# The two halves of a split weight in one buffer, at ten offsets: a TensorE-bound encoder on one core

## The chip, the core and the metric

One core of one Trainium2 chip runs the kernel. The metric is the time of one execution on the device, in microseconds (us). Two runs of the kernel before took 962.38 and 962.40 us, median 962.39. Engines are called as the profile calls them: PE (TensorE, matmuls), PEld (TensorE's weight loads), DVE (VectorE), ACT (ScalarE), POOL (GpSimd) and SP (SyncE, which issues the transfers).

## The reference

A trunk of two encoder layers over 256 tokens of width 1024, float32 throughout. In each layer the normed input is multiplied by one wide matrix, feeds four branches (latent attention, a short gated convolution, a convolution module with 31 taps, chunked spatial gating), and the branches are merged by sigmoid gates:

```
h = rms_norm(x, norm_mix_pre[l])
proj = h @ w_in[l]
...
merged = g[:, :, 0] * y_a + g[:, :, 1] * y_b + g[:, :, 2] * y_c + g[:, :, 3] * y_d
x = x + rms_norm(merged @ w_out[l], norm_mix_post[l])
h2 = rms_norm(x, norm_ffn_pre[l])
gu = h2 @ w_ffn_in[l]
f_g, f_u = jnp.split(gu, 2, axis=-1)
f = (jax.nn.silu(f_g) * f_u) @ w_ffn_out[l]
x = x + rms_norm(f, norm_ffn_post[l])
```

Nearly all of the work is products of the 256 tokens with some 83 MB of weights in each layer, each of which is read once.

## The kernel before, in words

**Weights come in units.** `unit_list` (line 46) cuts each layer's weights into 80 units of up to 128 x 2048 words. A unit is fetched by SP into a buffer `raw` (4 of them), and then split by `Weights.split` (line 345) into two float32r halves: ACT rounds `raw` to `hi` (line 356), DVE takes the rest, `lo = raw - hi` (line 357). There are five buffers for `hi` and five for `lo`, each of 2048 words, and unit number i uses the i-th of them in turn. The activations are split in the same way (`hth`/`htl` for the normed input, `fh`/`fl`, `mh`/`ml` and others for what follows).

**Products come in threes.** `group` (line 390) multiplies high by high, high by low and low by high into one bank of PSUM; each matmul has a weight load of its own (the stationary operand), and streams the other operand past it (the moving one, which is named first in the profile, as `pb<-hi,hth`). Two ways of use matter here:

- In most units the weights are moving: 512 words of `hi` or `lo` are streamed past 128 columns of activations. The first three units of a layer (`compressed`, line 659) stream 272 words at a time, and one unit (`w_uq`) 384.
- In the units of `w_in` with all 1024 rows (`b_unit`, line 534: 256 columns of one of the convolution, gating or short-convolution inputs) the weights are stationary: 128 columns of `hi` or `lo` are loaded, and 256 words of `hth` or `htl` streamed.

**Where the operands lie.** In the program as built, `hth`, `htl`, every `raw`, `hi` and `lo` buffer and every 512-word slot begins 64 bytes behind a multiple of 256 bytes in its partition. So a moving block of 512 or 256 words and the weights that are loaded for it begin at the same place in a line of 256 bytes: their distance, as it is called below, is 0 bytes modulo 256. Only the units of 544 columns depart from it: their blocks of 272 words are 1088 bytes long, and block k, half n begins 2176k + 1088n bytes into the buffer, so with three rows of blocks the distances run 0, 64, 128, 192, 0, 64, and with two (the third such unit) 0, 64, 128, 192.

**The order of the work** is written out by a planner in the kernel itself: it keeps a clock with an estimated cost for each instruction and picks, engine by engine, what is issued next (classes and functions from line 168 on; every ACT, DVE and POOL instruction is recorded at line 176). Side work (transposes, attention, the convolution) is slipped between the big products. Small columns of one to six words (`small`, line 287) go round through rings of eight buffers for each width.

Of the kernel before, what the change touches and what calls it, by code (L numbers as in the profile page):

```python
# [11 lines left out]
F32 = mybir.dt.float32  # L12
F32R = mybir.dt.float32r
# [5 lines left out]
P = 128  # L19
L = 2  # L20
D = 1024
# [10 lines left out]
EPS = 1e-6  # L32
NCOL = 148
UW = 2048
FIRST = 544

O_CQ, O_CKV, O_KR = 0, 256, 512
# [59 lines left out]
def hybrid_encoder(ctx: ExitStack, tc: tile.TileContext, wts, x_in, pos, invf, cols, rows, wst, out):  # L97
# [62 lines left out]
    class Engine:  # L160
        def __init__(self, eng, key, cost):
            self.eng, self.key, self.cost = eng, key, cost
# [102 lines left out]
    wp = ctx.enter_context(tc.tile_pool(name="wp", bufs=1))  # L265
    sb = ctx.enter_context(tc.tile_pool(name="sb", bufs=1))
    ps = ctx.enter_context(tc.tile_pool(name="ps", bufs=1, space=bass.MemoryType.PSUM))

    B_RAW, B_HI, B_SLOT, B_BIG, B_GAIN = 4, 5, 25, 2, 2
# [7 lines left out]
    def nm(s):  # L277
        cnt[0] += 1
        return f"{s}_{cnt[0]}"
# [5 lines left out]
        return sb.tile([P, D], F32, tag="big", name=nm(s), bufs=B_BIG)  # L285

    def small(n, s="c"):
        return sb.tile([P, n], F32, tag=f"c{n}", name=nm(s), bufs=8 if n < 8 else 4)

    rings = {"pb": [], "psd": []}  # L290

# [30 lines left out]
    units = unit_list()  # L322
# [3 lines left out]
        offs.append(offs[-1] + w)  # L326
    NU = len(units)

    class Weights:
        def __init__(self):  # L330
            self.nd = self.ns = self.n = self.nf = 0
# [2 lines left out]
        def load(self, i, t=0.0):  # L334
            l, u = divmod(i, NU)
            w, after = widths[u], t
            t = wp.tile([P, UW], F32, tag="raw", name=nm("raw"), bufs=B_RAW)
            o = (l * offs[-1] + offs[u]) * P
            src = wts[o : o + w * P].rearrange("(p w) -> p w", w=w)
            step = FIRST if i == 0 else w  # L340
            for c in range(0, w, step):
# [2 lines left out]

        def split(self, i):
            w = widths[i % NU]
            h = wp.tile([P, UW], F32R, tag="hi", name=nm("hi"), bufs=B_HI)
            lo = wp.tile([P, UW], F32R, tag="lo", name=nm("lo"), bufs=B_HI)
            raw = self.raw.pop(i)
            step = FIRST if i == 0 else 1024  # L350
            self.parts[i] = (h, lo)
            spans = [(c, min(w, c + step)) for c in range(0, w, step)]

            def rank():
                return 0 if i <= self.n + NEAR else 3

            for c, e in spans:
                act.copy(h[:, c:e], raw[:, c:e], rank=rank)
                dve.tensor_tensor(lo[:, c:e], raw[:, c:e], h[:, c:e], op=ALU.subtract, rank=rank, then=self.more if e == w else None)
# [89 lines left out]

    pii = sb.tile([P, T], I32, tag="pii", name="pii")  # L450
    fr = small(16, "fr")

    def tables():
# [5 lines left out]
    def rope_tables():  # L459
        pi = small(T, "pi")  # L460
        dve.tensor_copy(pi, pii)
        ang = small(T * 16, "ang")
        n = small(T * 16, "n")
        for t in range(T):
            dve.tensor_scalar(ang[:, t * 16 : (t + 1) * 16], fr, pi[:, t : t + 1], None, op0=ALU.mult)
        magic = 12582912.0
        dve.tensor_scalar(n, ang, float(np.float32(1.0 / (2 * math.pi))), None, op0=ALU.mult)
        dve.tensor_scalar(n, n, magic, None, op0=ALU.add)
        dve.tensor_scalar(n, n, magic, None, op0=ALU.subtract)
        c1 = 6.28125  # L470
        c2 = math.floor((2 * math.pi - c1) * 2**20) / 2**20
        c3 = 2 * math.pi - c1 - c2
        for c in (c1, c2, c3):
            dve.scalar_tensor_tensor(ang, n, -c, ang, op0=ALU.mult, op1=ALU.add)
        lim = 3.1415925
        dve.tensor_scalar(ang, ang, lim, -lim, op0=ALU.min, op1=ALU.max)
        act.activation(sin.rearrange("p t f -> p (t f)"), ang, AF.Sin)
        dve.scalar_tensor_tensor(n, ang, -1.0, ang, op0=ALU.mult, op1=ALU.max)
        dve.tensor_scalar(n, n, -1.0, math.pi / 2, op0=ALU.mult, op1=ALU.add)
        act.activation(cos.rearrange("p t f -> p (t f)"), n, AF.Sin)  # L480
# [4 lines left out]
    def pre_norm(t, g):  # L485
        h = big()
        ss = small(2)
        s1 = small(1)
        r = small(1)
        for j in range(2):  # L490
            c = slice(512 * j, 512 * (j + 1))
            act.activation(h[:, c], x[:, t, c], AF.Square, scale=D ** -0.5, accum_out=ss[:, j : j + 1], rank=FAST)
            if j == 0:
                pool.tensor_scalar(s1, ss[:, 0:1], EPS, None, op0=ALU.add, rank=FAST)
        rstd_of(r, ss[:, 1:2], s1, rank=FAST)
        for j in range(2):
            c = slice(512 * j, 512 * (j + 1))
            dve.scalar_tensor_tensor(h[:, c], x[:, t, c], r, g[:, c], op0=ALU.mult, op1=ALU.mult, rank=FAST)

        def turn():  # L500
            for j in range(2):
                yield need(h)
                b = sbank()
                transposes(b, [h[:, 512 * j + P * k : 512 * j + P * (k + 1)] for k in range(4)])
                bv = b.rearrange("p (k n) -> p k n", n=P)
                split(hth[:, t, 4 * j : 4 * j + 4, :], htl[:, t, 4 * j : 4 * j + 4, :], bv, FAST)

        return turn()
# [87 lines left out]
    def layer(l):  # L596
# [26 lines left out]
        def mla_tr(t, cn):  # L623
            yield need(cn)
            b = sbank()
            transposes(b, [cn[:, P * k : P * (k + 1)] for k in range(4)])
            for j in range(2):
                o = slice(t * P, (t + 1) * P)
                split(ft2(qc[j])[:, :, o], ft2(ql[j])[:, :, o], b[:, 256 * j : 256 * (j + 1)].rearrange("p (f n) -> p f n", f=2))
# [85 lines left out]
        def split_op(name, j, src):  # L715
            hi, lo = slot(F32R, name + "h"), slot(F32R, name + "l")
            split(hi, lo, src)
            ops[name][j] = (ft2(hi), ft2(lo))
# [481 lines left out]
```

## Time and profile before

| | before |
|---|---|
| median of two runs | 962.39 us |
| the profiled execution's own time | 962.84 us |
| its span, first to last instruction | 961.0 us |
| PE busy | 949.9 us (99%) |
| DVE busy | 669.8 us (70%) |
| ACT busy | 478.5 us (50%) |
| mean granted clock of TensorE | 0.998 of 2.4 GHz |

The profiled execution took 0.45 us longer than the median; 1.84 us of it lie outside the span. Matmuls are pipelined: a row of the profile gives a matmul's time from its start to the end that is modelled for it (389 ns for 512 columns), which overlaps the next one. What one matmul costs is read from the distance between two starts, so a stretch of equal matmuls is priced by its first and last start and their number.

### The profile page before, as it was taken

The page shows a single profiled execution, that of the slowest core. Times are in us where ns is not written, and L with a number is a line of the kernel's source. Part 1 is how long each engine was busy: PE and PEld are TensorE (multiplying, and loading weights), DVE is VectorE, ACT ScalarE, POOL GpSimd, SP SyncE. Part 2 cuts the span into 40 slices and gives each one's busy share as a digit, 9 for nine tenths or more (in the row PEclk, how much of TensorE's full clock was granted, in tenths as well). Part 3 has the DMA queues.
Part 4 walks back from the last instruction along what each step waited for, and adds up shares of the span by engine and source line. Part 5 has one row for each costly group of instructions (what it writes and reads, how often), then busy time and mean ns, then how long its engine had stood idle before and what let it go on. Part 6 is the DMA issues. An engine that isn't in the chain of part 4 may idle for free.

```text
span 961.0 us, 12988 instructions
## 1 busy us (share of the span) xinstructions
PE 949.9 (99%) x5098; PEld 821.4 (85%) x5098; DVE 669.8 (70%) x1018; ACT 478.5 (50%) x749; POOL 50.9 (5%) x95
## 2 busy tenths in 40 slices
PE   7999999999999999999999999999999999999997
PEld 7999988888888888888899999888888888888885
DVE  5978898898857655563387888798887675555432
ACT  6655654446435644443375655544454554444421
POOL 2200000000002000000041000000000110000000
PEclk9999999999999999999999999999999999999999
DMA  8754353565854555565268154455667366455601
GB/s 342 281 200 137 127 175 139 190 229 186 300 181 176 219 178 190 200 221 173 96 231 296 45 176 164 143 186 187 203 239 258 124 218 249 176 176 182 226 8 44
DMA packets 29869, 179.52 MB, mean 187 GB/s; under 512 B 3696, under 2 KB 3824, under 8 KB 10352
## 3 DMA queue, kind: packets, MB, share of 16 engines
q1 hardware_dynamic: 29808, 178.69, 52.3%
q8 instruction: 40, 0.66, 0.3%
q14 instruction: 21, 0.17, 0.0%
HBM read 177.63 MB, written 1.05 MB: 186 GB/s over the span
## 4 chain that ended last, share of the span: by engine, by line
PE 97%; DMA 1%; issue 1%; DVE 0%; SPq 0%; ACT 0%; POOL 0%; DVEq 0%; POOLq 0%
PE pb L256 77%; PE acc L256 12%; PE psd L260 4%; PE psd L256 2%; PE av L256 1%; DMA raw<-in_wts_dram 1%; SPq L317 0%; DVE lo L176 0%; POOL c L176 0%; ACT hi L176 0%; DVE x L176 0%; DVEq L1196 0%; ACT h L176 0%; POOLq L1196 0%; DVE htl L176 0%
## 5 line engine op out<-in xcount | busy, mean ns | idle before, releaser
L176 DVE TENSOR_TENSOR lo<-raw,hi 128x1024 fp32r<-128x1024 f32 (+4 forms) x321 | 374.5, 1202 | 137.6 <-ACT hi L176 137.5
L176 ACT CAST hi<-raw 128x1024 fp32r<-128x1024 f32 (+4 forms) x321 | 319.3, 1036 | 282.8 <-PE pb L256 132.6
L256 PE MATMUL pb<-hi,hth 128*128 128x512 f32 (+1 forms) x704 | 264.3, 387 | 0.7 <-ACT hth L176 0.5
L256 PE MATMUL pb<-lo,hth 128*128 128x512 f32 (+1 forms) x704 | 259.6, 381 | 0.5 <-DVE lo L176 0.5
L256 PE MATMUL pb<-hi,htl 128*128 128x512 f32 (+1 forms) x704 | 259.4, 381 | 0.4 <-DVE htl L176 0.4
L256 PEld LDWEIGHTS pb<-hi,htl 128*128 128x128 f32 x704 | 128.9, 188 | 26.0 <-DVE htl L176 0.6
L256 PEld LDWEIGHTS pb<-hi,hth 128*128 128x128 f32 x704 | 129.2, 188 | 25.4 <-ACT hi L176 0.7
L256 PEld LDWEIGHTS pb<-lo,hth 128*128 128x128 f32 x704 | 129.1, 188 | 24.5 <-DVE lo L176 0.7
L256 PE MATMUL pb<-hth,hi 128*128 128x256 f32 x384 | 109.9, 286 | 0.0
L256 PE MATMUL pb<-htl,hi 128*128 128x256 f32 x384 | 108.6, 283 | 0.0
L256 PE MATMUL pb<-hth,lo 128*128 128x256 f32 x384 | 108.6, 283 | 0.0
L176 DVE SCALAR_TENSOR_TENSOR yc<-zc,hcol,yc 128x241 f32<-128x241 f32 (+14 forms) x240 | 97.9, 472 | 0.0
L256 PEld LDWEIGHTS pb<-htl,hi 128*128 128x128 f32 x384 | 73.7, 192 | 0.3
L256 PEld LDWEIGHTS pb<-hth,hi 128*128 128x128 f32 x384 | 73.6, 192 | 0.3
L256 PEld LDWEIGHTS pb<-hth,lo 128*128 128x128 f32 x384 | 73.7, 192 | 0.0
L256 PE MATMUL acc<-hi,fh 128*128 128x512 f32 x176 | 68.8, 391 | 0.0
L256 PE MATMUL acc<-hi,fl 128*128 128x512 f32 x176 | 68.5, 389 | 0.0
L256 PE MATMUL acc<-lo,fh 128*128 128x512 f32 x176 | 68.5, 389 | 0.0
L256 PEld LDWEIGHTS acc<-hi,fl 128*128 128x128 f32 x176 | 33.0, 188 | 6.9
L256 PEld LDWEIGHTS acc<-lo,fh 128*128 128x128 f32 x176 | 33.0, 188 | 6.8
L256 PEld LDWEIGHTS acc<-hi,fh 128*128 128x128 f32 x176 | 33.0, 188 | 6.8
L176 POOL TENSOR_SCALAR c<-c 128x1 f32<-128x1 f32 (+1 forms) x20 | 10.7, 534 | 510.2 <-ACT sq L176 474.3
(161 smaller groups left out, 1018.1 us busy)
## 6 DMA issues: line engine op xcount, KB each, us to landing
raw<-in_wts_dram SPq DMA_DIRECT2D x152, 1024.0 KB, 4.8
brow<-in_rows_dram SPq DMA_DIRECT2D x24, 256.0 KB, 5.7
gain<-in_rows_dram SPq DMA_DIRECT2D x8, 512.0 KB, 6.5
raw<-in_wts_dram SPq DMA_DIRECT2D x3, 816.0 KB, 4.6
raw<-in_wts_dram SPq DMA_DIRECT2D x2, 768.0 KB, 6.0
raw<-in_wts_dram SPq DMA_DIRECT2D x2, 544.0 KB, 6.2
out_dram<-x SPq DMA_DIRECT2D x4, 256.0 KB, 2.1
raw<-in_wts_dram SPq DMA_DIRECT2D x3, 272.0 KB, 7.1
```

The source lines that it names most:

```text
L176: o.emit = lambda: f(*a, **k)
L256: nc.tensor.matmul(out, lhsT, rhs, **k)
L260: nc.tensor.transpose(out=out, in_=in_, identity=identity)
```

## The change

A unit's `hi` and `lo` now lie in one buffer `hl` of 2 x 2048 + 64 words, of which there are five. `hi` begins at an offset `at0`, and `lo` 2048 words behind it. The offset comes from a table by the number of the unit modulo five: 8, 12, 20, 24 or 28 words (32, 48, 80, 96 or 112 bytes) for the units that `b_unit` uses as stationary operand, and 2, 4, 12, 56 or 60 words (8, 16, 48, 224 or 240 bytes) for all others. The buffers themselves begin at the same place in a line of 256 bytes as before. The 1280 bytes more in each partition are made room for by rings of six buffers in place of eight for the small columns.

In the program as built, each engine has the same instructions in the same order as before, apart from waits. Since a buffer is now released as a whole, some of ACT's roundings wait for one to six matmuls more than before (those that read the `lo` of the same buffer last), and some of DVE's subtractions for 21 to 48 fewer. PE has eight waits more on matmuls of its own, of which each was issued at least 18 matmuls earlier. Some of the small columns on POOL, ACT and DVE now wait also for the reader of the column six places back in the ring.

```diff
@@ -32,6 +32,7 @@
 UW = 2048
+ROOM = 64
 FIRST = 544
@@ -285,7 +286,7 @@
     def small(n, s="c"):
-        return sb.tile([P, n], F32, tag=f"c{n}", name=nm(s), bufs=8 if n < 8 else 4)
+        return sb.tile([P, n], F32, tag=f"c{n}", name=nm(s), bufs=6 if n < 8 else 4)
@@ -326,6 +327,10 @@
     NU = len(units)
 
+    def phase(i):
+        src, r0, r1, _ = units[i % NU]
+        return ((8, 12, 20, 24, 28) if src == "w_in" and r1 - r0 == D else (2, 4, 12, 56, 60))[i % 5]
+
     class Weights:
@@ -344,8 +349,9 @@
         def split(self, i):
             w = widths[i % NU]
-            h = wp.tile([P, UW], F32R, tag="hi", name=nm("hi"), bufs=B_HI)
-            lo = wp.tile([P, UW], F32R, tag="lo", name=nm("lo"), bufs=B_HI)
+            both = wp.tile([P, 2 * UW + ROOM], F32R, tag="hl", name=nm("hl"), bufs=B_HI)
+            at0 = phase(i)
+            h, lo = both[:, at0 : at0 + UW], both[:, UW + at0 : 2 * UW + at0]
             raw = self.raw.pop(i)
```

## Rows read from the trace of the kernel before

**Rows 1.** The page: span, engines' busy time, clock by slices, chain that ended last.

```profile
span 961.0 us, 12988 instructions
...
PE 949.9 (99%) x5098; PEld 821.4 (85%) x5098; DVE 669.8 (70%) x1018; ACT 478.5 (50%) x749; POOL 50.9 (5%) x95
...
DVE  5978898898857655563387888798887675555432
...
PEclk9999999999999999999999999999999999999999
...
PE 97%; DMA 1%; issue 1%; DVE 0%; SPq 0%; ACT 0%; POOL 0%; DVEq 0%; POOLq 0%
```

**Rows 2.** PE's waits, whole run: us in total, times, longest.

```profile
PE psd L260 <- DVE h L176: 2.0, 1, 2.0
PE warm L260 <- POOL mhalf L176: 1.3, 1, 1.3
PE pb L256 <- DVE lo L176: 0.5, 1, 0.5
PE pb L256 <- ACT hth L176: 0.5, 1, 0.5
PE pb L256 <- DVE htl L176: 0.4, 1, 0.4
PE pb L256 <- ACT hi L176: 0.3, 1, 0.3
```

**Rows 3.** Groups of matmuls: count, busy us, mean ns, idle before.

```profile
L256 PE MATMUL pb<-hi,hth 128*128 128x512 f32 (+1 forms) x704 | 264.3, 387 | 0.7 <-ACT hth L176 0.5 <-ACT hi L176 0.3
...
L256 PE MATMUL pb<-hth,hi 128*128 128x256 f32 x384 | 109.9, 286 | 0.0
...
L256 PE MATMUL acc<-hi,fh 128*128 128x512 f32 x176 | 68.8, 391 | 0.0
...
L256 PE MATMUL pb<-hi,hth 128*128 128x272 f32 x64 | 10.5, 293 | 0.7 <-ACT hth L176 0.5 <-ACT hi L176 0.3
...
L260 PE MATMUL psd<-ident,f 128*128 128x128 f32 x88 | 11.9, 272 | 0.0
```

**Rows 4.** PE's timeline, 512 columns and 256: start us, us, instruction.

```profile
315.49 0.39 PE L256 MATMUL pb<-hi,hth 128*128 128x512 f32 x1
...
322.29 0.39 PE L256 MATMUL pb<-hi,hth 128*128 128x512 f32 x1
...
536.51 0.28 PE L256 MATMUL pb<-hth,lo 128*128 128x256 f32 x1
...
537.95 0.28 PE L256 MATMUL pb<-hth,lo 128*128 128x256 f32 x1
```

**Rows 5.** PE's timeline, 272 columns, third unit of layer 0.

```profile
25.34 0.67 PE L256 MATMUL pb<-hi,hth 128*128 128x272 f32 x4
25.84 0.66 PE L256 MATMUL pb<-hi,htl 128*128 128x272 f32 x4
26.34 0.66 PE L256 MATMUL pb<-lo,hth 128*128 128x272 f32 x4
26.84 0.39 PE L256 MATMUL pb<-hi,hth 128*128 128x512 f32 x1
```

**Rows 6.** PE's timeline behind four transposes in the feed-forward part.

```profile
311.60 0.60 PE L260 MATMUL psd<-ident,f 128*128 128x128 f32 x4
...
312.27 0.40 PE L256 MATMUL pb<-lo,hth 128*128 128x512 f32 x1
...
314.12 0.39 PE L256 MATMUL pb<-hi,hth 128*128 128x512 f32 x1
```

**Rows 7.** Attention scores: four records on PE's timeline, all 64 by tile.

```profile
104.65 1.03 PE L256 MATMUL psd<-kT,qT 96*128 96x256 f32 x4
...
L256 PE MATMUL psd<-kT,qT x64: 377/378/382, 104.7 to 631.0; 96*128 96x256 f32 x64
```

**Rows 8.** Groups of DVE and ACT by form, as in Rows 3.

```profile
L176 DVE TENSOR_TENSOR lo<-raw,hi 128x1024 fp32r<-128x1024 f32 x311 | 368.9, 1220 | 137.6 <-ACT hi L176 137.5
...
L176 DVE SCALAR_TENSOR_TENSOR yc<-zc,hcol,yc 128x255 f32<-128x255 f32 x16 | 6.8, 479 | 0.0
...
L176 DVE SCALAR_TENSOR_TENSOR yc<-zc,hcol,yc 128x254 f32<-128x254 f32 x16 | 6.6, 477 | 0.0
...
L176 ACT CAST hi<-raw 128x1024 fp32r<-128x1024 f32 x311 | 314.3, 1051 | 279.2 <-PE pb L256 132.6 <-issue 75.2 <-PE acc L256 36.3
```

## The prediction

> **What bounds the kernel now.** I read the page first, then PE's waits, then its timeline. PE is busy 949.9 of 961.0 us, the chain of work that ended last lies on it for 97%, and the clock is granted in full, the level of 2.4 GHz, in every slice [rows 1]. So the end moves only if PE's own stream gets shorter or longer. The list of waits says the same from the other side: all that PE waited for other engines is 5.0 us in six waits, of which the longest (2.0 and 1.3 us) are at the start [rows 2]. Weights that come late are not the matter, nor are ACT, DVE and the transfers.
>
> What then is in a matmul? A row's duration does not tell, since matmuls overlap; the spacing of starts does. From 315.49 to 322.29 us thirty matmuls of 512 columns start, one each 6.80 / 30 = 226.7 ns; 512 columns at 2.4 GHz are 213.3 ns, so 13.3 ns, or 32 cycles, are not streaming. Twelve of 256 columns take 1.44 us, 120.0 ns each, against 106.7: again 13.3 ns [rows 4]. A rest that does not grow with the columns is a price per matmul. How many pay it: the matmuls with a `hi` or `lo` operand are three kinds of 704, three of 176, and 672 of the same kinds from the other operands (mixing, four branches, the latent vectors), 3312 that stream weights, and three kinds of 384 that load them [rows 3], together 4464. Without the 192 of 272 columns that leaves **4272, and 4272 x 13.3 ns = 57 us**: the one reserve on the path that this change can touch.
>
> **Can the place of an operand change that rest?** Three rows bear on it, and they are the bounds.
>
> - Below: the attention scores. Four records of 256 columns span 1.03 us, the last takes 0.378 of it, so three starts are (1.03 - 0.378) / 3 = 217.3 ns apart [rows 7]. That is two cycles for a column (213.3 ns) and 4.0 ns of rest. They too load weights for each record, but stream at half the rate. So at most 4.0 ns of the 13.3 belong to changing weights, and 9.3 ns are a stall that comes with the full rate. A stall can be removed; that is the lower end, -9.3 ns.
> - Nearest: the 272-column matmuls, the only ones whose moving block does not lie at distance 0 from the weights. In the third unit the distance runs through 0, 64, 128 and 192 bytes, and three groups of four take 26.84 - 25.34 = 1.50 us, 125.0 ns each [rows 5]. Less 113.3 ns of streaming that is 11.7 ns, 28 cycles in place of 32. If the one in four at distance 0 pays its 32, the other three average 26.7 cycles, 5.3 fewer: -2.2 ns. So the distance does count, and distance 0 is none of the good ones.
> - Above: what the rest becomes when the stream is out of step. Behind four transposes, eight starts take 314.12 - 312.27 = 1.85 us, 231.3 ns each, 4.6 ns over the settled spacing at the very same addresses [rows 6]. That is the upper end, +4.6 ns.
>
> The new distances are none that the trace shows. For the units that stream weights they are +8, +16, +48, -32 and -16 bytes, for the stationary ones the weights lie 32 to 112 bytes ahead of the moving block; no unit keeps distance 0. I start from the nearest row, -2.2 ns. In its stretch the distance changes from one matmul to the next, so the stream cannot settle, while in the changed kernel all matmuls of a unit have one distance. What settling is worth is 4.6 ns in the 512-column row [rows 4, 6]; so the nearest row, settled, is somewhere between -2.2 and -6.8 ns. I take **-4.0 ns**, below the middle, because settling may not have been lacking in full: 4272 x 4.0 = **17.1 us**.
>
> A rule speaks against any gain, so it is weighed here. The Trainium skill, "SBUF — State Buffer", section "SBUF: two separate sides", says that TensorE has ports of its own, and a second independent one for weight loads, and that it never waits for anyone; by it no distance between two operands matters, the sum is 0 and the time stays 962. The 28 cycles for the mixed distances against 32 [rows 4, 5] do not agree with it in full, though 1.7 ns is little to go by.
>
> **The rest of the change** costs nothing that I can find.
>
> - Writes at new places: ACT's rounding and DVE's subtraction write the shifted halves. DVE's convolution, whose operands begin one word further at each tap, takes 479 ns for 255 elements and 477 for 254 [rows 8]: odd or even start, no step. So I take 0. If there were one, DVE has 961 - 670 = 291 us free, and the 311 big subtractions take 369 us [rows 1, 8]; they would have to become 79% longer before DVE, over the whole run, were the bound.
> - One buffer for both halves: ACT's rounding waits up to six matmuls longer. The longest kind, six of 272 columns at 125 ns [rows 5], is 0.75 us, for a buffer that is wanted units later; PE waited for `hi` once, for 0.3 us [rows 2]. What is queued behind the rounding on ACT are evictions and other roundings; DVE waits for them, and PE behind DVE, which it did for `lo` once, 0.5 us. I take 0, at the most 1 us.
> - PE's eight waits for itself: each looks 18 or more matmuls back, 18 x 120 ns = 2.2 us or more [rows 4], long past a matmul's 0.4 us. 0.
> - Rings of six: attention's columns pass through the ring at one per step, and PE's list has no wait for POOL but at the start [rows 2]. 0.
> - Transfers are the same, issued by the same events.
>
> If PE gains 17 us, what is late next? DVE, at nine tenths or more in three of the first ten slices [rows 1]; 2% more there still fits. So the sum is 962.84 - 17.1 = 945.7 us for the profiled execution. The median of the runs shown stands 0.45 us below that execution: **945 us**.
>
> **The rivals.**
>
> - *The stall goes away* (0.22). If the new distances avoid what the full-rate stream trips over, the rest falls to that of the scores: 4272 x 9.3 ns = 40 us, 923 us. The case reaches from the forecast's edge, 933, to where the loads themselves set the pace: transposes, which stream little, follow at (0.60 - 0.272) / 3 = 109 ns [rows 3, 6], 11 ns under the 120 of 256 columns, and 4272 x 11 = 47 us would leave 915. For it: the scores show the stall is no fixed price of a weight load [rows 7]. Against: no fp32r row shows less than 28 cycles. The Trainium skill, "TensorE: Matmul & The Clock Gate", section "Back-to-back issue gap", has columns / 2.4 GHz + 2.5 ns for matmuls whose spacing is not set by loads; by it 10.8 ns would go and the time be 916, but the spacing here differs from it by just that, 226.7 against 215.8 [rows 4].
> - *Distance does nothing* (0.16): the 28 cycles of the third unit come from its odd block length, not from its distances. 962 us. This is also the case that the change does not do what it says to the stream. For it: one short stretch, and 1.7 ns. Against: the rest is 32 cycles for blocks of 256 and 512 alike.
> - *The stream never settles* (0.12). At the new distances the state behind a transpose [rows 6] becomes the rule: 4272 x 4.6 ns = 20 us, 982 us. It is slower by 2% from 19.2 us / 4272 = 4.5 ns a matmul on. For it: the same addresses give both spacings, so the state depends on how loads and stream fall in time, and 8-byte offsets shift that. Against: mixed distances, which should be the worst, gave less, not more [rows 5].
>
> **The numbers.** The forecast has 0.50 and its own range from -2.2 to -6.8 ns: 953 to 933. Two per cent, about what a measurement of this kernel can tell from no change, are 19.2 us: under 943.1 is faster, over 981.6 slower. The forecast puts 0.19 under 943.1 and 0.31 above it. Faster: 0.19 + 0.22 = 0.41. Within: 0.31 + 0.16 and 0.04 of the unsettled case that stays below 2%, 0.51. Slower: 0.08. The range goes from 918 (leaving out some 0.06 of the case of the vanished stall) to 966 (leaving out the unsettled case, 0.12): it takes in the unchanged time and the 1 us that late buffers may cost.
>
> **What would show it.** In the changed kernel's timeline, thirty settled 512-column matmuls should start some 222 to 223 ns apart, and those of 256 columns 116; 217 and 111 would mean the stall is gone, 226.7 and 120 that distance is nothing, 231 that the stream does not settle. Spacing should be constant within a unit and may differ between the five offsets. The scores' 217 ns must not move. Groups of `hi` and `lo` on ACT and DVE should keep 1051 and 1220 ns, and PE's waits stay near 5 us. The prediction is wrong if the spacing stays and the time moves, for then a wait has moved it; or if only one of the two kinds of use changes.

## The result, and the profile after

The changed kernel takes 979.07 us (two runs, 978.65 and 979.48) against 962.39: 1.0174 of the time before, 95% interval 1.0158 to 1.019. It is 1.7% slower, outside the range of the prediction, and on the other side of the unchanged time.

The page of the changed kernel has the same picture at the top as [rows 1]: PE bounds it for 97%, and the clock is granted in full.

```profile
span 976.9 us, 13007 instructions
...
PE 967.3 (99%) x5098; PEld 824.8 (84%) x5098; DVE 670.5 (69%) x1018; ACT 478.1 (49%) x749; POOL 49.6 (5%) x95
...
PEclk9999999999999999999999999999999999999999
...
PE 97%; DMA 1%; issue 1%; DVE 0%; SPq 0%; ACT 0%; POOL 0%; DVEq 0%; POOLq 0%
```

PE's waits, as in [rows 2]: no new one has come, and the 2.0 us at the start are gone, 3.3 us in all in place of 5.0. So no buffer comes late.

```profile
PE warm L261 <- POOL mhalf L177: 1.3, 1, 1.3
PE pb L257 <- ACT hth L177: 0.9, 1, 0.9
PE pb L257 <- DVE hl L177: 0.5, 1, 0.5
PE pb L257 <- DVE htl L177: 0.3, 1, 0.3
PE pb L257 <- ACT hl L177: 0.3, 1, 0.3
```

DVE's and ACT's split of the weights, by form, keep the durations of [rows 8]: writing at the new places costs nothing.

```profile
L177 DVE TENSOR_TENSOR hl<-raw,hl 128x1024 fp32r<-128x1024 f32 x311 | 368.9, 1220 | 143.8 <-ACT hl L177 143.8
...
L177 ACT CAST hl<-raw 128x1024 fp32r<-128x1024 f32 x311 | 314.0, 1050 | 291.5 <-PE pb L257 149.2 <-issue 77.7 <-PE acc L257 38.1
```

The time is in PE's own stream. Its timeline, three places: 512 columns in the feed-forward part; the third unit of 272; four records of the scores.

```profile
318.64 0.40 PE L257 MATMUL pb<-hl,htl 128*128 128x512 f32 x1
...
325.65 0.39 PE L257 MATMUL pb<-hl,htl 128*128 128x512 f32 x1
...
24.30 0.67 PE L257 MATMUL pb<-hl,hth 128*128 128x272 f32 x4
24.80 0.66 PE L257 MATMUL pb<-hl,htl 128*128 128x272 f32 x4
25.30 1.13 PE L257 MATMUL pb<-hl,hth 128*128 128x272 f32 x6
...
103.64 1.03 PE L257 MATMUL psd<-kT,qT 96*128 96x256 f32 x4
```

Between the first two rows lie thirty starts: 7.01 / 30 = 233.7 ns, where [rows 4] have 226.7. The 272-column blocks still start 0.50 / 4 = 125.0 ns apart, as in [rows 5], though their distances are now 48, 112, 176 and 240 bytes. The scores are as in [rows 7].

Over the whole trace (all starts of a matmul followed by one of the same width, without those that wait) the spacing is:

| columns streamed | starts | before, ns | after, ns | in all |
|---|---|---|---|---|
| 512 | 2955 | 227.2 | 233.2 | 3072 x 6.0 = +18.4 us |
| 256 (weights loaded) | 1132 | 119.9 | 119.2 | 1152 x -0.7 = -0.8 us |
| 272 | 178 | 125.6 | 126.7 | 192 x 1.1 = +0.2 us |

That is +17.8 us. PE's waits are 1.7 us shorter (5.0 to 3.3), which leaves 16.1; the spans differ by 976.9 - 961.0 = 15.9.

The 48 matmuls of 384 columns (`w_uq`) are not in the table: they go from 173.7 to 175.8 ns (42 starts), 0.1 us in all.

### The profile page after: what moved, and what is told of

It is laid out like the page before. It is cut to its first block, busy times and chain, and to the rows that moved or that the text cites. A ratio compares the mean times of both kernels' runs of the same rounds, so it can differ in the third digit from the quotient of the medians.

```text
span 976.9 us, 13007 instructions
## 1 busy us (share of the span) xinstructions
PE 967.3 (99%) x5098; PEld 824.8 (84%) x5098; DVE 670.5 (69%) x1018; ACT 478.1 (49%) x749; POOL 49.6 (5%) x95
## 4 chain that ended last, share of the span: by engine, by line
PE 97%; DMA 1%; issue 1%; DVE 0%; SPq 0%; ACT 0%; POOL 0%; DVEq 0%; POOLq 0%
PE pb L257 78%; PE acc L257 12%; PE psd L261 4%; PE psd L257 2%; PE av L257 1%; DMA raw<-in_wts_dram 1%; SPq L318 0%; DVE hl L177 0%; POOL c L177 0%; ACT hl L177 0%; DVE x L177 0%; DVEq L1202 0%; ACT h L177 0%; POOLq L1202 0%; DVE htl L177 0%
## 5 line engine op out<-in xcount | busy, mean ns | idle before, releaser
L177 DVE TENSOR_TENSOR hl<-raw,hl 128x1024 fp32r<-128x1024 f32 (+4 forms) x321 | 374.5, 1202 | 144.2 <-ACT hl L177 144.1
L177 ACT CAST hl<-raw 128x1024 fp32r<-128x1024 f32 (+4 forms) x321 | 319.0, 1035 | 294.5 <-PE pb L257 149.2
L257 PE MATMUL pb<-hl,hth 128*128 128x512 f32 (+1 forms) x1408 | 425.6, 389 | 1.6 <-ACT hth L177 0.9
L257 PEld LDWEIGHTS pb<-hl,hth 128*128 128x128 f32 x1408 | 256.1, 189 | 56.2 <-ACT hth L177 1.1
L257 PE MATMUL pb<-hl,htl 128*128 128x512 f32 (+1 forms) x704 | 263.4, 386 | 0.3 <-DVE htl L177 0.3
L257 PEld LDWEIGHTS pb<-hl,htl 128*128 128x128 f32 x704 | 129.7, 189 | 29.0 <-DVE htl L177 0.6
L257 PE MATMUL pb<-hth,hl 128*128 128x256 f32 x768 | 140.6, 284 | 0.0
L257 PEld LDWEIGHTS pb<-hth,hl 128*128 128x128 f32 x768 | 119.2, 189 | 0.3
L257 PE MATMUL acc<-hl,fh 128*128 128x512 f32 x352 | 110.9, 396 | 0.0
L257 PE MATMUL pb<-htl,hl 128*128 128x256 f32 x384 | 108.3, 282 | 0.0
```

The source lines that it names most:

```text
L177: o.emit = lambda: f(*a, **k)
L257: nc.tensor.matmul(out, lhsT, rhs, **k)
```

## The experiments

Two theories at first. *Distance*: what counts is where the streamed block lies against the one that is loaded meanwhile. *Alignment*: a block that begins off 64 bytes costs more, at 16 cycles for one more line. A third that had to go first: the waits and rings of the new layout.

**The layout without offsets, and each half of the table alone.**

```diff
 def phase(i):
+    return 0                                         # one_buffer
+    ((0, 0, 0, 0, 0) if src == "w_in" ... else (2, 4, 12, 56, 60))   # moving_only
+    ((8, 12, 20, 24, 28) if src == "w_in" ... else (0, 0, 0, 0, 0))  # loads_only
```

> The changed kernel with every offset 0: one buffer for both halves and rings of six stay, the places in a line of 256 bytes are those of before. If the offsets alone cost the time (both theories, line and distance), 962 to 963 us, settled spacing 226.7 ns for 512 columns and 120.0 for 256. If the later releases, the eight waits or the rings of six cost it, 975 to 979 us at 226.7 ns.

> Offsets of 8, 16, 48, 224 and 240 bytes for the units that are streamed, 0 for those that are loaded. The loss is put on the streamed units (3072 matmuls of 512 columns at 233 ns in place of 227, some 18 us) and a small gain on the loaded ones (some 1 us): 979 to 981 us, 512 columns at 232 to 234 ns, 256 at 120.0. If the two kinds of use affect each other, less.

> Offsets of 32 to 112 bytes for the units that are loaded, 0 for those that are streamed. 512 columns back at 226.7 ns, 256 columns at 117 to 120 as in the changed kernel: 961 to 962 us, a gain of 0 to 1.5 us on before.

Measured: 962.41 us without offsets (ratio 0.9998, 0.9989 to 1.0007), 979.31 with those of the streamed units alone (1.0175, 1.016 to 1.019), 960.74 with those of the loaded ones alone (0.9982, 0.9973 to 0.9992). Spacing of 512 and of 256 columns: 227.2 and 119.9 ns; 232.9 and 119.9; 227.2 and 118.6. So the layout is free, the whole loss belongs to the streamed units, and the loaded ones gain 1.7 us.

**All sixteen places.** The offset of the n-th unit of its kind is 16 x (n mod 16) bytes.

```diff
-        return (...)[i % 5]
...
+        return 4 * (nth % 16)
```

> Both kinds of units go through the sixteen offsets 0, 16, 32, ... 240 bytes, so that the spacing is read for each. Line theory (a streamed block of 512 words that begins off a 64-byte line touches 33 lines in place of 32, at 16 cycles a line): 226.7 ns at 0, 64, 128 and 192 bytes, 233.3 at the twelve others, whatever the distance from the loaded block; some 975 us. Distance theory (what counts is where the streamed block lies against the block loaded meanwhile, modulo 256 bytes): a curve of its own that has no such period of 64 bytes, with some offset under 224 ns, since three quarters of the 272-column blocks seemed to gain by their distances of 64 to 192 bytes.

Measured: 975.23 us, one run. Mean spacing by offset in ns, from 160 to 205 starts each (512 columns) and 44 to 96 (256, from one or two units for each offset):

| bytes | 0 | 16 | 32 | 48 | 64 | 80 | 96 | 112 | 128 | 144 | 160 | 176 | 192 | 208 | 224 | 240 |
|---|---|---|---|---|---|---|---|---|---|---|---|---|---|---|---|---|
| 512 streamed | 228.6 | 231.6 | 233.4 | 232.1 | 229.6 | 231.1 | 233.8 | 230.8 | 232.7 | 233.1 | 233.9 | 232.9 | 233.1 | 234.6 | 233.0 | 231.5 |
| 256 past loaded | 119.9 | 118.4 | 118.4 | 117.8 | 113.6 | 118.7 | 118.8 | 119.8 | 118.8 | 119.7 | 119.6 | 118.1 | 117.9 | 116.6 | 116.7 | 119.9 |

The lines of 64 bytes do not show: 128 and 192 bytes cost as much as any. The distance theory's hope for a good offset falls too: for 512 columns **0 is the best on average, and all others are worse**. For 256 columns 0 is the worst but for a tie.

A mean can hide two spacings. At 240 bytes the mean of 231.5 ns is mixed of stretches at 233.3, at 236.6, and at the 226.7 ns of distance 0, which three of the eight units keep (unit 75 of layer 0, units 39 and 71 of layer 1, counted from 0). Two units of layer 1, 39 and 55, both at 240 bytes:

```profile
731.24 0.61 PE L257 MATMUL pb<-hl,cfh 128*128 128x512 f32 x2
...
735.32 0.61 PE L257 MATMUL pb<-hl,cfh 128*128 128x512 f32 x2
...
826.92 0.64 PE L257 MATMUL pb<-hl,hth 128*128 128x512 f32 x2
...
829.76 0.64 PE L257 MATMUL pb<-hl,hth 128*128 128x512 f32 x2
```

Eighteen starts take 4.08 us in the first, 226.7 ns each, and twelve take 2.84 us in the second, 236.7. Unit 55 starts at 227 ns too, and goes over to 234 and 239 in turn behind eight transposes. So at one distance there can be several *rhythms*, spacings or short patterns of spacings that repeat until something interrupts them; none that was seen for 512 columns is under the 227 ns of distance 0.

**Distance against alignment.** A column of 8 bytes, which takes 32, is put ahead of everything (pad_all), or behind hth and htl (pad_weights), in the kernel before.

```diff
+    padt = cp.tile([P, 2], F32, name="padt")      # pad_all
+    pool.memset(padt, 0.0)
     mhalf = cp.tile([P, 2], F32, name="mhalf")
...
+    padw = wp.tile([P, 2], F32, tag="padw", name="padw", bufs=1)   # pad_weights
+    pool.memset(padw, 0.0)
     units = unit_list()
```

> The kernel before, with one small unused column ahead, which moves every operand of a matmul by 32 bytes: all lie off a line of 64 bytes, all distances stay 0. Distance theory: nothing changes, 962 to 963 us, 226.7 ns for 512 columns, 120.0 for 256. Alignment theory (what costs is a block that does not begin on 64 bytes): some 233 ns for 512 columns as at 32 bytes in the sweep, 980 us or more.

> The kernel before, with the column between hth/htl and all that follows: raw, hi, lo and the 512-word slots move by 32 bytes, hth and htl stay. The streamed block begins off 64 bytes everywhere, but the distance is 32 bytes only where hth or htl is loaded (1920 matmuls of 512 columns) and 0 where a slot is (1152). Distance theory: 233.4 ns for the first, 226.7 for the second, loaded weights at 118.3; 962.4 + 1920 x 6.7 ns - 1152 x 1.6 ns = 973 us. Alignment theory: 233 for both, 980 us.

Measured: 962.21 us (ratio 1.0, 0.999 to 1.0009) and 971.78 (1.0093, 1.0077 to 1.011). Timeline of pad_all, then of pad_weights, first past htl and then past fh:

```profile
315.41 0.39 PE L256 MATMUL pb<-hi,hth 128*128 128x512 f32 x1
...
322.21 0.39 PE L256 MATMUL pb<-hi,hth 128*128 128x512 f32 x1
```

```profile
316.42 0.39 PE L256 MATMUL pb<-hi,htl 128*128 128x512 f32 x1
...
323.42 0.39 PE L256 MATMUL pb<-hi,htl 128*128 128x512 f32 x1
...
434.25 0.39 PE L256 MATMUL acc<-hi,fh 128*128 128x512 f32 x1
...
441.05 0.39 PE L256 MATMUL acc<-hi,fh 128*128 128x512 f32 x1
```

With everything displaced alike, thirty starts take 6.80 us, 226.7 ns. With the weights displaced against hth they take 7.00 us, 233.3 ns, and in the same execution, from the same displaced buffers, 6.80 us again against fh, which is displaced with them. Over all starts: 233.2 past hth and htl, 227.2 past the slots, and 118.3 for the loaded weights. So the place of the streamed block in a line of 64 bytes means nothing here; its distance to what is loaded does. (Wherever weights are streamed, the block that a stream runs past and the one that is loaded meanwhile lie at the same place in a line of 256 bytes, so which of the two counts is not shown.)

**Modulo what?** All units at 256 bytes.

```diff
+        return 64
```

> All units at an offset of 256 bytes. If places count modulo 256 bytes, as the table's top of 240 suggests, this is distance 0: 226.7 and 120.0 ns, 962 to 963 us. If they count modulo 512 or more, 230 to 235 ns as at the other offsets, 972 to 980 us.

Measured: 961.92 us (0.9995, 0.9986 to 1.0005), 227.2 and 119.9 ns. 256 bytes count as 0, and no smaller multiple of 16 in the sweep does: the distance counts modulo 256 bytes.

**One displaced block of three.** hi at 0, lo at 16 x (n mod 16) bytes, in both kinds of units.

```diff
+            h, lo = both[:, :UW], both[:, UW + at0 : 2 * UW + at0]
```

> hi at offset 0 in every unit, lo at 0, 16, 32, ... 240 bytes by the unit's number, so that of three streamed blocks two have distance 0 and one has not. If each matmul pays for its own distance, blocks of hi stay at 226.7 ns and blocks of lo take the 230 to 235 of the sweep, some 966 us. If one shifted block upsets the lock of all three, all three lengthen, 970 us or more; or an offset shows under 224 ns, which no offset of both halves did.

Measured: 973.01 us, one run. In streamed units whose lo is displaced, the blocks of hi, at distance 0, take 231.4 ns on average, those of lo 232.8. A matmul does not pay for its own distance alone: one displaced block puts the three out of step.

**Is it a better kernel, then, with the loaded units alone displaced?** At 64 bytes, which stood at 113.6 ns in the sweep, and with lo alone at 144. The 112.7 ns that the expectation has for it is the mean of the lo blocks, one start in three; the whole unit stood at 115.6 in the last run, which would promise 957.4 us in place of 954.

```diff
+        return 16 if src == "w_in" and r1 - r0 == D else 0     # loads_64
+        return 36 if src == "w_in" and r1 - r0 == D else 0     # loads_lo_144, hi at 0
```

> Offset 64 bytes for the units that are loaded, 0 for those that are streamed, as the sweep would choose. If the spacing belongs to the offset, 256 columns start 113.6 ns apart in all 1152 and the time is 962.4 - 1152 x 6.3 ns = 955.2 us. If the 113.6 of the sweep was an accident of its five units, 118 to 120 ns and 960 to 962 us.

> Streamed units at 0; loaded units with hi at 0 and lo 144 bytes on, which stood at 112.7 ns in the one unit of the last sweep that had it. If the pair of distances sets the spacing, 1152 x 7.3 ns go: 954 us. If it was only one of several rhythms that a unit can fall into by how it is entered, as 64 bytes turned out, 117 to 120 ns and 959 to 962 us.

Measured: 959.40 us (0.9967, 0.9954 to 0.998) and 958.99 (0.9965, 0.9952 to 0.9977), both faster than either kernel, and both only by the lesser gain. The same offset of 64 bytes, in the sweep and in loads_64:

```profile
60.77 0.28 PE L257 MATMUL pb<-htl,hl 128*128 128x256 f32 x1
...
64.85 0.28 PE L257 MATMUL pb<-htl,hl 128*128 128x256 f32 x1
```

```profile
59.60 0.28 PE L257 MATMUL pb<-htl,hl 128*128 128x256 f32 x1
...
63.84 0.28 PE L257 MATMUL pb<-htl,hl 128*128 128x256 f32 x1
```

Thirty-six starts take 4.08 us there, 113.3 ns each, and 4.24 here, 117.8. The spacing is constant in both stretches. But loads_64 has both rhythms itself, at the one offset that all its loaded units share. Unit 16 of layer 0 and the next:

```profile
103.03 1.03 PE L257 MATMUL psd<-kT,qT 96*128 96x256 f32 x4
...
104.14 0.39 PE L257 MATMUL pb<-hth,hl 128*128 128x256 f32 x2
...
108.22 0.39 PE L257 MATMUL pb<-hth,hl 128*128 128x256 f32 x2
...
110.47 1.03 PE L257 MATMUL psd<-kT,qT 96*128 96x256 f32 x4
...
111.57 0.40 PE L257 MATMUL pb<-hth,hl 128*128 128x256 f32 x2
...
115.81 0.40 PE L257 MATMUL pb<-hth,hl 128*128 128x256 f32 x2
```

Behind the first four scores thirty-six starts take 4.08 us again, 113.3 ns; behind the next four, 4.24. Of the 24 loaded units, 22 stand at 117.6 to 118.0 ns, unit 16 of layer 0 at 113.3 and unit 17 of layer 1 at 113.8, and the rhythm changes only where attention's matmuls cut in. loads_lo_144 is alike: nine units at 115.6 to 116.4, fifteen at 117.7 to 118.1. So one distance has more than one steady rhythm, and a stream can leave one for another when it is interrupted; what in the way in decides was not tried.

**Half the loads.** The middle products load and compute 64 columns of the stationary operand in place of 128, so half of the output rows lack those terms; in the kernel before and in the changed one. They are 1512 of the 512-column matmuls and 864 of the 256-column ones.

```diff
+            q = slice(0, P if i == 0 or (last and i == n - 1) else 64)
+            pe.matmul(o[q], lh[:, q], rh, ...)
```

> The kernel before; in the products of line 390 the middle terms (half of those matmuls) load and compute only 64 of the 128 columns of the stationary operand, so half of the output rows lack those terms. The streamed block is the same. If the 32 cycles of rest are stolen from the stream by the block that is loaded meanwhile, the spacing ahead of a half load falls from 226.7 to about 220 ns (16 cycles) and from 120.0 to about 113, some 12 us in all; the last products (acc), which are left whole, stay at 226.7. If the rest is a price of changing weights whatever is loaded, nothing moves: 962 us.

> The same in the changed kernel, at its offsets. If the loss by distance (48 cycles for 32) is a clash of the streamed block with the loaded one, half the load clashes less: 225 to 229 ns ahead of a half load against 233, the whole acc products stay at 233. If distance upsets the stream itself, 233 everywhere and 979 us.

Measured: 961.62 and 971.85 us, one run each. In the first, a half block of 256 columns followed by another starts it 114.0 ns later, a whole one followed by a whole one 119.7, the number that was expected of a load that takes from the stream. But the gain goes with the matmul that runs, not with the load behind it: a half one followed by a whole one starts it 113.4 ns later (46 starts), a whole one followed by a half one 117.5 (44). And 512 columns between half loads stand at 229.9, where the kernel before has 227.2: the shorter load loses the good rhythm. In the changed kernel they go from 232.5 between whole loads to 230.2. The acc products, left whole, stay at 226.9 and 233.0. So for 512 columns the rest is not stolen in proportion to what is loaded, and the theory fails there; for 256 it is not shown, since the run halves what is computed together with what is loaded.

**Length or operand?** 512 columns lose by a distance where the weights are streamed, 256 gain where they are loaded. The middle matmuls of 512 are cut in two of 256, with a load for each.

```diff
...
+                    for c in (slice(0, 256), slice(256, 512)):
+                        pe.matmul(o[:, c], l, r[:, c], **f)
```

> The kernel before; in the products of line 390 the middle matmuls of 512 columns are issued as two of 256 with the same stationary operand loaded for each. At distance 0 each half should cost 120.0 ns as the 256 columns of the loaded units do: some 1450 x 13.3 ns = 19 us more, 981 us. It is the reference for the next run.

> The same in the changed kernel. If the sign hangs on the length of the stream, halves of displaced weights start 117 to 119 ns apart, below the 120 at distance 0, and the whole blocks left beside them still at 233. If it hangs on which operand is displaced, halves take 124 to 127 ns, so that each pays the 6 ns or so that a whole block pays, and the time is some 1005 us.

Measured: 983.37 us at distance 0 and 982.20 with the table's offsets, one run each; 1512 matmuls are cut. Timeline of the second, past hth and htl:

```profile
325.39 0.62 PE L257 MATMUL pb<-hl,hth 128*128 128x512 f32 x2
325.85 0.39 PE L257 MATMUL pb<-hl,htl 128*128 128x512 f32 x1
326.08 0.63 PE L257 MATMUL pb<-hl,hth 128*128 128x256 f32 x4
326.54 0.40 PE L257 MATMUL pb<-hl,htl 128*128 128x256 f32 x2
326.78 0.63 PE L257 MATMUL pb<-hl,hth 128*128 128x256 f32 x4
327.24 0.40 PE L257 MATMUL pb<-hl,htl 128*128 128x256 f32 x2
327.48 0.60 PE L261 MATMUL psd<-ident,f 128*128 128x128 f32 x4
```

From 326.08 to 327.48 us twelve halves start, 116.7 ns each, out of a unit whose whole blocks, just before, take (326.08 - 325.39) / 3 = 230 ns. Over all starts a half behind a half stands at 117.9 ns with offsets and 119.2 without, a whole block behind a whole one beside them at 232.3 and 232.5, and the whole acc products, with no halves near, at 233.0 and 226.9. The sign hangs on the **length of the stream**, not on the operand that is displaced; the 384 columns, with +2.1 ns, lie between. Each half has a load of its own, so a shorter stream is here also a more frequent load, and no run parts the two. The whole blocks beside halves lose their good rhythm at distance 0 too, so for whole blocks only the acc products compare.

## Why the prediction was wrong

- **What bounds the kernel** was right: PE's stream alone, a rest of 13.3 ns a matmul, 57 us in all, and no wait. The changed kernel's 15.9 us are in that rest, within 0.2 us by the table and the waits above. That 979.07 us lies within 2% of the time before, to which the prediction gave 0.51, is no merit: all but 0.04 of that was a small gain or none.
- **That distance changes the rest** was right, and pad_all against pad_weights show it. The Trainium skill's rule ("SBUF — State Buffer", section "SBUF: two separate sides") that TensorE never waits for anyone at its ports, read as the prediction read it, would have kept 962. So read it does not agree with the 971.78 and 962.21 us for the two places of one pad, and the measurement decides; that a port waits is not shown.
- **The step that failed** is the price: "I start from the nearest row, -2.2 ns", and with it "distance 0 is none of the good ones". It was +6.0 ns for 512 columns. The nearest row was a block of 272 columns, and the sign hangs on the length: blocks of 256 gain by a distance, those of 512 lose. Nor does the row hold what was read out of it. With four other distances its spacing is again 125.0 ns, and over all 272-column blocks of the kernel before those at distance 0, 64, 128 and 192 bytes start 126.0, 125.5, 126.5 and 123.0 ns apart (30 to 57 starts each): the one at 0 pays 12.7 ns above its columns, 30 cycles in place of the 32 that the sum gave it, and of the other three only the one at 192 gains more than 0.5 ns. That 256 and 512 columns had the same 32 cycles was true at distance 0 only.
- **"The nearest row, settled, is somewhere between -2.2 and -6.8 ns"** took unsettled for a surcharge that goes away. The sweep shows it the other way round: at distance 0 the stream falls into its best steady rhythm (226.7), at others it settles as well, but at 229 to 237 (save for the three units at 240 bytes). In the changed kernel's rows the 233.7 holds over thirty starts.
- **The loaded units** were forecast with the same -4.0 ns; they gave -0.7 with the table as a whole, -1.3 alone. Right in sign, a third or less in size.
- **The rival on the other side** (+4.6 ns, 982 us, chance 0.12) had the place, nearly the price (+6.0 on 3072 matmuls, where it put 4.6 on 4272) and the mechanism in part: it is not that the stream never settles, but that it settles on a longer rhythm. Its chance was set by "mixed distances gave less, not more", which was the row of 272 again. "The stall goes away" did not happen: no offset brought 512 columns under the 227 ns of distance 0. For 256 columns half of it went, 120.0 to 113.3 ns, in the few units that fell into that rhythm.
- **The parts at nothing** (writes at new places, one buffer, PE's eight waits, rings of six) were right: 962.41 us for all of them together.

## What to carry to other kernels

When PE is full and its clock is granted, price a matmul by the spacing of starts and ask what the rest above its columns hangs on; here it hangs on the distance between the streamed and the loaded block, modulo 256 bytes, and on the stream's length, so a row for another length is no price. Keep operands that PE uses together at equal places modulo 256 bytes where 512 columns of float32r are streamed: a pad of 32 bytes between the loaded `hth`/`htl` and the buffers behind them cost 0.9%, ahead of all nothing. A mean over units may mix rhythms, so look at single units before an offset is chosen by it: 64 bytes promised 955 us and gave 959.40. If offsets are to be tried, try each kind of use alone: half of this table was a small gain (0.9982), and hidden by the other half.

## What the runs showed of the hardware that was not expected

- Streams of 512 float32r columns with a load for each have a rest of 32 cycles at 2.4 GHz at distance 0 and, in the sweep, 39 to 51 on average at the fifteen other multiples of 16 bytes; streams of 256 have 32 at distance 0 and, there, 17 to 32 at others.
- One distance has several steady rhythms: 113.3 and 117.8 ns for 256 columns at 64 bytes, in one kernel; 226.7, 233.3 and 236.6 for 512 at 240 bytes. They mostly repeat: in the changed kernel, units of the two layers with the same offset and place show the same means, from unit 7 on within 0.2 ns (233.3, 236.0, 234.2 and 231.9 ns in units 28 to 31 of both). But unit 6, with 48 bytes in both layers, stands at 123.2 ns in the first and 117.8 in the second.
- With distance, cutting a stream in two is nearly free: two halves take 2 x 117.9 = 235.8 ns, a whole block 233; the run with the halves took 3.1 us more than the changed kernel, 982.20 against 979.07, where the kernel before lost 21.4, 983.37 against 961.97 beside it.
- The Trainium skill, "TensorE: Matmul & The Clock Gate", section "Back-to-back issue gap", gives columns / 2.4 GHz + 2.5 ns as the gap of an isolated matmul, with no budget for weight loads. No steady stretch of 512 columns here came near its 215.8 ns; the steady 113.3 ns for 256 is within 4.1 ns of its 109.2.
- Why the length decides, and what the streamed and the loaded block share, stays open: at distance 0 half the load helps 256 columns and harms 512, so it is no simple theft of reads.
